# The PSUM ring of the late projections and the odd layer: five banks in five steps

## The chip, the cores and the metric

The kernel runs on one core of a Trainium2 chip. Its time is the device time of one execution in microseconds (us). A core has a matrix engine (TensorE, PE in the profile; PEld is its weight load), a vector engine (VectorE, DVE), a scalar engine (ScalarE, ACT), a general engine (GpSimd, POOL), a queue of DMA issues (SyncE, SP), and DMA engines beside them. Matmuls write their sums to PSUM, eight banks of 512 fp32 columns on 128 partitions; DVE and ACT read the sums from there.

## The reference

One step of a two-layer network on 1024 latent tokens and 256 context tokens of width 1024 (DEPTH = 2). Layer 0 is the even layer (attention), layer 1 the odd one (Fourier mixing); then a final norm.

```python
for l in range(DEPTH):
    hc = modulate(rms_norm(xc, norm_g[l]), shc, scc)      # context
    hl = modulate(rms_norm(xl, norm_g[l]), shl, scl)      # latent
    if l % 2 == 0:   # combined projection; global and windowed attention; SiLU gates; output projection
        yc, ka, va, kb, vb = even_ctx(hc, ...)
        yl = even_lat(hl, ...)
    else:
        yc = odd_mix(hc, odd_w_in[i], odd_w_out[i])
        yl = odd_mix(hl, odd_w_in[i], odd_w_out[i])
    xc = xc + gtc * yc
    xl = xl + gtl[:, None] * yl

def odd_mix(h, w_in, w_out):
    u, gate = jnp.split(h @ w_in, 2, axis=-1)
    return (fourier_mix(u) * jax.nn.silu(gate)) @ w_out   # fourier_mix: Re(FFT2) over positions and 256 channels
```

All values are fp32. The kernel splits each fp32 operand into a high and a low part and makes three matmuls of each product.

## The kernel before

The ten tiles of 128 tokens are projected, normalised and rotated; the queries go through DRAM (`qd`); the attention runs unit by unit (tile, head group, pair of heads), and a filler puts projections and gates between the units. When the last unit is done, `late[0]` becomes true (L1515), and what the filler still holds is run to its end (`fl_.drain()`, L1517).

From there on the sums of every large product come from one function, `next_bank`, which takes the next tag of a ring:

```python
BANKS = {"s": 3, "t": 3, "a": 1, "g": 1}
RING = ("g", "s", "a", "s")
...
    ring = deque(RING)

    def next_bank(name):
        ring.rotate(-1)
        return bank(ring[-1], name)
```

The tag "g" stands for one PSUM bank, "a" for one, "s" for three that are given out as they come free, and "t" for three that serve transposes and small sums and are not in the ring. A tile (one 512-column sum) owns its bank from its first matmul to the last instruction that reads it; the next tile of that tag waits until then.

Walking the program gives 91 calls of `next_bank`, in this order. I number them from 0.

- 0 to 13: `oz`, the output projection of the even layer for the seven rows left at L1515 (6, 3, 7, 1, 5, 8, 9), two halves each (L1304); 24 matmuls a tile, read by DVE at L1308.
- 14 to 37: the gates of the odd layer, L1529 to L1584, four steps `c` of two channel tiles `ct`. For each `ct` a tile `g1E` and a tile `g1O` (L1539, 24 matmuls of 512 columns, read by ACT at L1545 and DVE at L1546, L1547 and L1549); at the end of each `c` two tiles `g1c` (L1559, 24 matmuls of 256 columns, read by ACT at L1562 and DVE at L1564 and L1565). In the last `c` the two small sums `ad12p` (L420) of `r2.finish("g")` (L1580) stand between the last `g1O` (call 35) and the two last `g1c` (calls 36 and 37); they ask for the tag "g" by name, outside the ring (L433).
- 38 to 57: `u`, four passes `n` of five tiles (L1805); 24 matmuls a tile over eight chunks `k` of 128 channels. Chunks 0 to 3 and 4 to 7 use weights that are loaded from `wd` (L1607) and split into a high part (L316, ACT) and a low part (L322, POOL). Read by ACT at L1813 and DVE at L1814.
- 58 to 69: `pcc`, `pc`, `ps`, the position sums of the Fourier mixing (L1828, L1854).
- 70 to 90: `of`, the output projection of the odd layer and the final norm (L1304, L1924).

The order of the instructions on each engine is not the program's. A planner (`schedule_with_timeline_sim=True`, L2053) goes through them with its own estimate of time and puts on an engine the earliest instruction of the program whose inputs and whose bank it thinks ready. The engines then run their queues strictly in that order. So a change of banks can move matmuls, evictions and DMA issues of the stages behind it.

Of the kernel before, what the change touches and what calls it, by code (L numbers as in the profile page):

```python
# [82 lines left out]
E_WL, E_VH, E_KEV, E_QEV = "p", "d", "a", "ad"  # L83
BANKS = {"s": 3, "t": 3, "a": 1, "g": 1}
ALIAS = {}
RING = ("g", "s", "a", "s")


class Buf:
# [57 lines left out]
def hybrid_step(ctx: ExitStack, tc: tile.TileContext, I, O):  # L147
# [37 lines left out]

    ring = deque(RING)

# [1873 lines left out]
```

## Time and profile before

| what | value |
|---|---|
| median of 3 runs | 1179.93 us (1179.76 to 1182.26) |
| profiled execution | 1181.93 us, of which its instructions span 1180.1 us |
| mean granted TensorE clock in the profiled execution | 0.995 |
| busy, of the span | PE 98%, PEld 88%, DVE 70%, ACT 48%, POOL 28% |
| matmuls | 8120 |
| stretch in which the ring is in use | about 764 to 1173 us |

The share of PE is made of matmuls whose ends are modelled, so it tells where PE stood still, not how close it is to its peak. The table of stages in the prediction is read in the same way: what a stage can give is its length less PE's busy time in it. Columns of the stage view: stretch, length, then busy us and number of instructions of PE, PEld, DVE, ACT and POOL, the granted TensorE clock, the share of the DMA engines and GB/s.

### The profile page before, as it was taken

The numbers are of one execution on the slowest core, as the hardware profiler recorded it, in microseconds if no ns is written. First come the engines' busy times: TensorE is split into PE (matmuls) and PEld (weight loads), VectorE is DVE, ScalarE is ACT, GpSimd is POOL, SyncE is SP. The second block draws the span as 40 slices with busy tenths as digits, with TensorE's granted clock in tenths as the row PEclk, the third lists the DMA queues.
The fourth block names the chain that finished last, engine by engine and source line by source line (L and its number), as shares of the span: only waits on it lengthen the run. The fifth ranks groups of instructions, "written<-read, shape, count | busy, mean of one in ns | idle before, by whom it ended". The sixth has DMA issues, their size and how long they took to land.

```text
span 1180.1 us, 22034 instructions
## 1 busy us (share of the span) xinstructions
PE 1151.1 (98%) x8120; PEld 1035.5 (88%) x8120; DVE 829.7 (70%) x1996; ACT 570.2 (48%) x1149; POOL 329.8 (28%) x293
## 2 busy tenths in 40 slices
PE   9998999999999999999999989999999999999997
PEld 8797999999999998899989878887777889998886
DVE  3589787877777776678888877776765962468543
ACT  4343466565656655556666674432363234342211
POOL 2345733512222230010110035365221226200001
PEclk9999999999999999999999999999999999999999
DMA  9977412323532232344352587784214426364321
GB/s 368 371 275 256 129 62 68 97 83 101 151 90 79 77 97 85 94 127 117 78 154 78 158 227 211 232 238 162 90 46 143 151 98 181 100 213 146 125 107 54
DMA packets 112592, 168.80 MB, mean 143 GB/s; under 512 B 25946, under 2 KB 63574, under 8 KB 112484
## 3 DMA queue, kind: packets, MB, share of 16 engines
q1 hardware_dynamic: 109972, 158.74, 42.6%
q0 software_dynamic: 2368, 8.39, 2.4%
q8 instruction: 64, 1.05, 0.4%
q14 instruction: 44, 0.36, 0.1%
q10 hardware_dynamic: 144, 0.26, 0.1%
HBM read 123.19 MB, written 44.16 MB: 142 GB/s over the span
## 4 chain that ended last, share of the span: by engine, by line
PE 70%; DMA 13%; DVE 8%; issue 3%; POOL 2%; ACT 2%; SPq 1%; POOLq 0%; DVEq 0%; ACTq 0%
PE of L296 9%; PE av L1114 9%; PE pt L1108 8%; PE ga L296 8%; PE q L296 8%; PE sL L989 5%; PE u L296 5%; PE g1O L296 3%; PE kv L296 3%; PE sC L989 2%; PE g1E L296 2%; PE oz L296 2%; DMA u<-i_x 2%; DMA wd<-u 2%; PE g1c L296 1%
## 5 line engine op out<-in xcount | busy, mean ns | idle before, releaser
L1111 DVE TENSOR_TENSOR pt<-pt,pt 128x512 fp32r<-128x512 f32 (+1 forms) x264 | 170.9, 658 | 40.5 <-ACT pt L316 39.5
L316 ACT ACTIVATE pt<-pt 128x512 fp32r<-128x512 f32 (+1 forms) x265 | 147.5, 576 | 101.8 <-PE pt L1108 56.2
L1114 PE MATMUL av<-pt,u 128*128 128x256 f32 x1008 | 167.5, 290 | 1.4 <-DVE e L1125 0.8
L1108 PE MATMUL pt<-identr,p 128*128 128x128 f32 x1008 | 157.2, 273 | 1.5 <-ACT p L1030 0.8
L296 PE MATMUL q<-w,u 128*128 128x256 f32 x960 | 145.1, 287 | 0.5 <-ACT e L559 0.5
L1114 PEld LDWEIGHTS av<-pt,u 128*128 128x128 f32 x1008 | 139.1, 190 | 5.0 <-DVE e L1125 1.0
L296 PEld LDWEIGHTS q<-w,u 128*128 128x128 f32 x960 | 127.2, 189 | 5.5 <-ACT e L559 0.7
L1030 ACT ACTIVATE p<-p,nm 128x1280 f32<-128x1280 f32 (+1 forms) x80 | 95.4, 1193 | 68.2 <-DVE p L1023 68.0
L1108 PEld LDWEIGHTS pt<-identr,p 128*128 128x128 f32 x1008 | 119.7, 141 | 8.1 <-ACT p L1030 1.0
L296 PE MATMUL ga<-u,w 128*128 128x512 f32 (+1 forms) x576 | 124.4, 360 | 0.8 <-DVE byp L1085 0.5
L296 PEld LDWEIGHTS ga<-u,w 128*128 128x128 f32 x576 | 93.8, 188 | 15.4 <-ACT pt L316 1.2
L322 POOL TENSOR_TENSOR w<-h,w 128x512 fp32r<-128x512 f32 x38 | 50.0, 1331 | 134.6 <-DVE w L318 106.6
L989 PE MATMUL sL<-u,q 128*128 128x512 f32 x256 | 82.3, 409 | 0.0
L1030 ACT ACTIVATE p<-p,NM 128x640 f32<-128x640 f32 (+2 forms) x80 | 59.2, 740 | 31.5 <-DVE p L1023 31.2
L989 PE MATMUL sC<-u,q 128*128 128x256 f32 x320 | 62.1, 294 | 2.3 <-DMA q<-qd 2.0
L1023 DVE TENSOR_SCALAR_CACHE_REDUCE p<-sL 128x512 f32<-128x512 f32 x64 | 43.8, 685 | 22.3 <-PE sL L989 14.0
L1023 DVE TENSOR_SCALAR_CACHE_REDUCE p<-sL,nm 128x512 f32<-128x512 f32 x64 | 47.7, 745 | 13.9 <-PE sL L989 12.8
L296 PE MATMUL oz<-u,w 128*128 128x512 f32 x192 | 56.4, 399 | 0.4 <-DVE e L1125 0.4
L759 POOL TENSOR_TENSOR h<-h,rope 128x512 f32<-128x512 f32 (+1 forms) x18 | 21.6, 1199 | 121.4 <-ACT h L842 79.2
L989 PEld LDWEIGHTS sC<-u,q 128*128 128x128 f32 x320 | 48.8, 189 | 5.9 <-issue 2.6
L322 POOL TENSOR_TENSOR u<-h,u 128x512 fp32r<-128x512 f32 x16 | 21.0, 1323 | 109.1 <-ACT u L316 81.2
L296 PE MATMUL of<-u,u 128*128 128x512 f32 x150 | 48.2, 393 | 0.0
(735 smaller groups left out, 2590.7 us busy)
## 6 DMA issues: line engine op xcount, KB each, us to landing
q<-qd SPq DMA_DIRECT2D x80, 256.0 KB
h<-i_w_in SPq DMA_DIRECT2D x40, 256.0 KB
h<-i_w_out SPq DMA_DIRECT2D x32, 256.0 KB
p<-i_ada_s SPq DMA_DIRECT2D x11, 512.0 KB
qd<-pt SPq DMA_DIRECT2D x20, 256.0 KB
qd<-q SPq DMA_DIRECT2D x18, 256.0 KB
w<-i_wuT SPq DMA_DIRECT2D x8, 512.0 KB
u<-i_x SPq DMA_DIRECT2D x8, 512.0 KB
```

Of the source, the lines that this page charges most:

```text
L296: last = pe.matmul(out, a, b, start=i == 0, stop=i == n - 1)
L316: return act.activation(out, in_, AF.Copy)
L322: return pick("lo" + lc, lc).tensor_sub(dst_l, src, dst_h)
L759: pick("rope", XE["rope"]).tensor_mul(t1.rearrange("p t h (b c) -> p t (h b) c", b=2), y.rearrange("p t h (b c) -> p t (h b) c", b=2), cb)
L989: pe.matmul(ps, q_at(q, s, hc), keys, start=s == 0, stop=s == 1)
L1023: dve.tensor_scalar(p[i][:, end[i] : end[i] + n], ps, sign, last[i], op0=ALU.mult, op1=ALU.min, accum_out=c)
L1030: act.activation(p[i][:, 0 : end[i]], p[i][:, 0 : end[i]], AF.Exp, bias=last[i], scale=-1.0, accum_out=SU[:, t, hd + i, 0:1],)
L1108: pe.transpose(tp[:, jj * 256 + i * P : jj * 256 + i * P + P], p[i][:, off : off + P], ident)
L1111: dve.tensor_sub(pt[:, 1, 0:n], tp[:, 0:n], pt[:, 0, 0:n])
L1114: pe.matmul(acc, vv, pt[:, s, jj * 256 : jj * 256 + 256], start=c + jj + s == 0, stop=c + jj == nt - 1 and s == 1,)
```

## The change

One constant gets a fifth step:

```diff
-RING = ("g", "s", "a", "s")
+RING = ("g", "s", "a", "s", "s")
```

Before, calls 0, 4, 8, ... take "g", calls 2, 6, 10, ... take "a", and every second call takes one of the three banks of "s". A bank of "g" or "a" comes back after four calls, a bank of "s" after six on average. Now "g" has calls 0, 5, 10, ..., "a" has calls 2, 7, 12, ..., and the other three of each five take "s": every bank comes back after five calls. The number of banks, the sums, the number of instructions and the DMAs stay the same.

## The prediction

> **What bounds the kernel now.** I read the page first, for the share of PE, then the view of stages, for where PE stands still once the ring is in use.
>
> ```profile
> span 1180.1 us, 22034 instructions
> PE 1151.1 (98%) x8120; PEld 1035.5 (88%) x8120; DVE 829.7 (70%) x1996; ACT 570.2 (48%) x1149; POOL 329.8 (28%) x293
> ```
>
> ```profile
> 770.00:850.00 80.00, 79.26 (x371) 64.49 (x370) 57.73 (x76) 22.39 (x44) 41.14 (x23) 1.00 0.52 167
> 850.00:910.00 60.00, 56.92 (x299) 46.06 (x298) 36.47 (x80) 32.81 (x74) 17.45 (x15) 1.00 0.26 88
> 910.00:980.00 70.00, 70.00 (x385) 59.79 (x384) 54.04 (x100) 20.69 (x39) 18.73 (x15) 1.00 0.40 131
> 980.00:990.00 10.00, 8.58 (x70) 8.20 (x69) 2.06 (x6) 3.94 (x9) 6.61 (x9) 1.00 0.73 219
> 990.00:1045.00 55.00, 55.00 (x517) 53.24 (x516) 22.73 (x75) 19.86 (x57) 16.99 (x13) 1.00 0.38 116
> 1045.00:1172.75 127.75, 127.75 (x644) 107.71 (x644) 77.83 (x133) 32.78 (x61) 7.73 (x11) 1.00 0.38 133
> ```
>
> The reader is to see that PE bounds every stage that uses the ring. Length less busy time leaves 0.74 us idle in 770 to 850, 3.08 in 850 to 910, 1.42 in 980 to 990, and nothing elsewhere. The change removes no instruction, so it can give at most these 5.24 us, and only the part of them that is a wait for a bank, or could be filled if another bank were free. The waits of PE after 765 us name them (who waited, for whom, us in all, times, longest):
>
> ```profile
> PE u L296 <- ACT u L316: 1.3, 1, 1.3
> PE g1c L296 <- ACT u L1330: 0.9, 2, 0.5
> PE g1E L296 <- DVE h L1565: 0.9, 1, 0.9
> ```
>
> Only the third is a wait for a bank as such: a `g1E` tile waits for the last reader of a `g1c` tile (L1565). The first is a wait for weights (L316 splits them), and what matters there is whether PE has other work.
>
> **The change part by part.** *The wait at 908 us.* It is call 22 (`g1E3`, tag "a") waiting for call 18 (`g1c0`, "a"). In the new ring call 22 still has "a", but the tile before it there is call 17 (`g1O1`), drained early.
>
> ```profile
> 906.91 0.28 PE L296 MATMUL g1c<-u,u 128*128 128x256 f32 x1
> 908.05 0.93 PE L296 MATMUL g1E<-w,u 128*128 128x512 f32 x3 [0.87 <-DVE h L1565]
> ```
>
> I count nothing for it all the same. When PE stops at 906.91 all five banks are taken: calls 18 and 19 (`g1c`, which wait for the context's transposes) and three finished tiles of the step `c` = 1. Before, these three are calls 20, 21 and 23, and 22 comes last; after, they are 20, 21 and 22, and 23, on an "s" bank, comes last and waits for the same readers. The work of three 24-matmul tiles is the same. What goes is the place of the wait, not its length. Bounds: all of it goes (0.87 less), or nothing; I take nothing, because the five banks are full in both orders.
>
> *The wait at 982 us.* Here PE runs out of ready matmuls before the second half of the first `u` weights is split:
>
> ```profile
> 969.62 1.09 PE L420 MATMUL ad12p<-h,ones 128*2 128x512 f32 x4
> 970.55 0.40 PE L296 MATMUL g1c<-u,u 128*128 128x256 f32 x2
> 973.39 0.28 PE L296 MATMUL u<-w,w 128*128 128x258 f32 x1
> 981.38 0.28 PE L296 MATMUL g1c<-u,u 128*128 128x256 f32 x1
> 982.93 0.63 PE L296 MATMUL u<-u,u 128*128 128x258 f32 x3 [1.27 <-ACT u L316]
> 983.71 0.36 PE L296 MATMUL u<-w,w 128*128 128x258 f32 x1
> ```
>
> The 24 matmuls of a `g1c` tile from 970.55 to 973.39 give 0.118 us a matmul. So PE's work ends at 981.38 + 0.12 = 981.50, and it starts again at 982.93: 1.43 us lost. It then does three matmuls (to 983.39) and waits until 983.71, 0.32 us, for call 40 (`u02`, "g"), whose bank is held by call 36 (`g1c6`, "g") until its reader is through:
>
> ```profile
> 983.28 0.28 DVE L1565 TENSOR_TENSOR h<-g1c,h 128x128 f32<-128x128 f32 x1
> ```
>
> Together 1.75 us. What PE lacked were banks: of the five `u` tiles only calls 38, 39 and 41 had run their first chunks (0 to 3, 12 matmuls, 1.42 us each). Call 40 stood behind `g1c6`, and call 42 ("a") behind call 38 ("a"), which needs the late weights itself. In the new ring call 36 has an "s" bank and call 37 has "a"; call 40 is behind `ad12p` alone, and call 42 behind call 37, the other `g1c` tile. Then the first chunks of calls 40 and 42 are ready too: 24 matmuls, 2.84 us, more than the 1.75 us lost. If the planner puts them ahead, PE has work until 981.50 + 2.84 = 984.34.
>
> *What the new ring adds there.* "g" now also has call 35, `g1O7`, the tile just before `ad12p`, which asks for "g" by name. Before, the tile ahead of `ad12p` on "g" was call 32 (`g1E6`), drained with the first row; now it is `g1O7`, drained with the second:
>
> ```profile
> 958.35 0.41 DVE L1547 TENSOR_TENSOR h<-g1E,h 128x256 f32<-128x256 f32 x1
> 971.09 0.16 DVE L1549 TENSOR_SCALAR h<-g1O 128x1 f32<-128x1 f32 x1
> ```
>
> So `ad12p` cannot start at 969.62 any more, but at 971.25 at the earliest: 1.63 us later. PE fills that time with calls 36 and 37 if they stand ahead in its queue. But others wait for `ad12p`, in this order: the DMA issue of `wd` pieces on SP, the landing, POOL, then SP again with the piece of the late weights, its landing, and the split:
>
> ```profile
> SPq L1607 <- PE ad12p L420: 8.8, 3, 5.5
> ```
>
> ```profile
> 970.74 5.72 SPq L1607 DMA_DIRECT2D h<-wd  x4
> 976.56 0.46 SPq L1555 DMA_DIRECT2D g1d<-u  x1
> 977.11 0.39 SPq L1607 DMA_DIRECT2D w<-wd  x1
> ```
>
> ```profile
> 973.69 0.10 POOL L1609 MEMSET h<- 128x4 f32 x1 [7.69 <-DMA h<-wd]
> 973.80 2.28 POOL L322 TENSOR_TENSOR h<-u,h 128x512 fp32r<-128x512 f32 x1
> 982.95 1.30 POOL L322 TENSOR_TENSOR u<-w,u 128x516 fp32r<-128x516 f32 x1
> ```
>
> ```profile
> 982.24 0.63 ACT L316 ACTIVATE u<-w 128x516 fp32r<-128x516 f32 x1 [4.09 <-DMA w<-wd]
> ```
>
> SP stands for 8.8 us behind `ad12p` between 965 and 975 us; the first of its four `h<-wd` issues at 970.74 starts POOL's memset at 973.69, POOL's 2.28 us finish the operand of the last `ad12p` matmul, and the piece `w<-wd` is issued at 977.11 behind all that. If the whole chain moves by 1.63 us, the high parts come at 982.87 + 1.63 = 984.50 and the low parts at 984.25 + 1.63 = 985.88. PE, with work until 984.34, waits 0.16 us, runs five matmuls of high parts (0.59 us) and waits 0.79 us for the low ones: 0.95 us idle in place of 1.75, a gain of 0.80. If the chain does not move, the gain is 1.75; if it moves and nothing is filled in, PE idles 1.63 us longer. I take the gain of 0.80: the wait for `g1O7` follows from the ring alone, and the rows show SP waiting for `ad12p`. The filling matmuls hide the wait; without them the next thing late is the low part.
>
> *The rest.* `oz` changes banks from call 4 on, but PE is idle 0.74 us in that stage, and its one bank wait there is for the last reader of an attention sum (L1125) on "a", which call 2 has in both rings:
>
> ```profile
> PE oz L296 <- DVE e L1125: 0.4, 1, 0.4
> ```
> The position sums change too: `ps3` (call 69) now comes after `pc1` (call 64) on "s", and `pc3` goes ahead of it. PE has `of` matmuls to run there and stands still nowhere after 990 us, so I count nothing. Bounds for the planner's rearrangements in 770 to 910: all 0.74 + 3.08 us of idle time gone, or, as the nearest row for a loss, one more wait like the 1.63 us one.
>
> The sum is −0.80 us on the profiled execution's 1181.93 us (span 1180.1, so 1.83 us lie around it), that is 1181.1. That execution is 2.00 us above the median of 1179.93; the same 0.80 us off the median gives **1179.1 us**.
>
> **The rivals.**
>
> *Faster.* The chain does not move, because the planner puts `w<-wd` ahead of what waits for `ad12p`, and the order at 908 us loses its wait as well: 1.75 + 0.87 = 2.62 us, 1177.3. For it: both waits are named in the rows. Against it: the full banks at 906.91 and SP's 8.8 us.
>
> *Nothing happens.* PE's queue has the same stalls in other places and the late weights set 982.93 as before: 1179.9. For it: the number of banks is the same, and the largest wait is for weights, not for a bank.
>
> *Slower.* The chain moves by 1.63 us and the planner, which goes by its own estimate, does not put calls 40 and 42 ahead. Then PE idles 1.43 + 1.63 = 3.06 us in one piece. What such a piece does to the clock the trace shows once, earlier:
>
> ```profile
> 749.50:753.08 3.58, 1.57 (x10) 1.20 (x11) 3.57 (x12) 3.32 (x8) 0.45 (x1) 1.00 0.95 286
> 753.08:756.49 3.41, 3.41 (x16) 3.21 (x15) 3.38 (x9) 3.36 (x9) 0.27 (x1) 0.50 0.16 50
> 981.00:984.40 3.40, 1.98 (x15) 1.60 (x14) 0.49 (x2) 2.15 (x5) 3.32 (x5) 1.00 1.07 314
> ```
>
> After a stretch with PE busy 1.57 of 3.58 us the granted clock was 0.50 for 3.41 us; around the present wait, with 1.98 of 3.40, it stayed at 1.00. So somewhere between 1.4 and 2.0 us of idle time in such a stretch the clock halves, and 3.06 us are past that. Half a clock for 3.41 us costs 1.71 us of matmuls: 1.63 + 1.71 = 3.34 us, 1183.3. It decides as soon as less than about 1 us of the 2.84 us of filling work is ahead in the queue.
>
> A page of the Trainium skill ("TensorE: Matmul & The Clock Gate", section "What's actually happening") has a stricter rule: the clock falls to half after at least one idle window of about 3.4 us. By that rule 3.06 us would not halve it, and the slower case would be 1179.93 + 1.63 = 1181.6, within 0.2%. The trace does not agree: at 753 us the clock fell after a stretch in which PE was busy for 1.57 of 3.58 us. So I keep the price with the halved clock.
>
> **How the numbers follow.** Forecast (filled, chain moved) 0.40, nothing 0.12, faster 0.25, slower 0.23. 0.2% is 2.36 us, about what a measurement of this kernel can tell from no change; the forecast and the second rival lie within it, 1177.3 and 1183.3 outside. So faster 0.25, same 0.52, slower 0.23. The likeliest time is 1179.1. The range runs from 1176.6, the faster case with 0.74 us of the idle time of 770 to 850 gone as well, to 1183.4, the slower case; cases of both signs hold much of the chance, and the forecast's own range is 1178.2 (gain 1.75) to 1179.9.
>
> **What would show it.** In the changed trace: `ad12p` at 971.3 or later behind or amid two `g1c` tiles; 60 matmuls of `u` on chunks 0 to 3 (now 36) before the first one that waits for L316; idle time in 980 to 990 under 1 us; a wait of about 0.9 us for L1565 near 907, now ahead of a `g1O` tile. I am wrong if `ad12p` still starts right behind `g1O7`, if `w<-wd` is issued at 977.1 or before, if a stretch at 0.50 clock follows 985 us, or if the stages from 770 to 910 change by over 1 us.

## The result, and the profile after

The changed kernel takes 1191.15 us (median of 5 runs, 1189.5 to 1191.73) against 1181.75 us for the kernel before in the same session (5 runs, 1179.76 to 1186.27): a ratio of 1.0076, with an interval of 1.0054 to 1.0097. It is slower by some 9 us, and above the upper end of the predicted range. The profiled execution took 1191.73 us. Ratios, here and below, leave out two executions of later kernels (1892.57 us of e2 and 1255.45 us of e4), whose mean granted clock was 0.556 and 0.849. The page of the changed kernel begins:

```profile
span 1189.9 us, 22037 instructions
PE 1154.1 (97%) x8120; PEld 1039.0 (87%) x8120; DVE 832.3 (70%) x1996; ACT 570.3 (48%) x1149; POOL 327.9 (28%) x293
```

The work is the same (8120 matmuls), so the 9.8 us of extra span are time in which PE stood still or was clocked down. The view of stages of the changed kernel has the columns used before:

```profile
770.00:850.00 80.00, 75.82 (x349) 61.96 (x348) 61.04 (x76) 21.51 (x40) 41.87 (x24) 0.98 0.53 174
850.00:910.00 60.00, 59.28 (x312) 48.81 (x310) 34.30 (x71) 32.20 (x70) 18.11 (x15) 1.00 0.26 86
910.00:980.00 70.00, 68.52 (x354) 58.08 (x354) 54.56 (x106) 19.80 (x41) 16.14 (x12) 0.98 0.35 117
980.00:990.00 10.00, 10.00 (x78) 9.02 (x76) 3.08 (x7) 4.67 (x10) 4.33 (x6) 1.00 0.81 247
990.00:1045.00 55.00, 50.53 (x469) 48.06 (x469) 20.73 (x67) 18.90 (x53) 19.82 (x21) 1.00 0.37 110
```

Two stages that had no idle time to speak of now have 4.18 us (770 to 850, before 0.74) and 4.47 us (990 to 1045, before 0). The idle time that the change was to remove (980 to 990, before 1.42) is gone, also in the changed kernel's own time, which is 6.22 us behind at that place: PE's first stop after 980 us comes at 1000.67. The waits of PE after 765 us name the new ones (who waited, for whom, us in all, times, longest):

```profile
PE eoE L1341 <- DVE p L1442: 4.1, 1, 4.1
PE u L296 <- ACT u L316: 2.5, 1, 2.5
PE u L296 <- DVE nyr L1816: 1.4, 1, 1.4
...
PE g1O L296 <- DVE h L1565: 0.9, 1, 0.9
PE u L296 <- POOL u L322: 0.6, 1, 0.6
```

For what follows I put the trace's matmuls against the kernel's own list of instructions, which gives each its tile, and cut the time at the same four matmuls in every run: the first of `oz60` (call 0), the last of the `oz` tiles, the last of `g1O7` (call 35), the last of the `u` tiles. Before: 764.25, 850.92, 969.40, 1044.37. After: 765.57, 857.09, 975.62, 1054.15. So the changed kernel is 1.32 us behind when the ring begins, where both kernels still have the same order of instructions on PE; it loses 4.85 us in the `oz` stretch (91.52 for 86.67), 0.05 in the gates (118.53 for 118.48), 3.56 in the `u` stretch (78.53 for 74.97) and nothing behind it. 1.32 + 4.85 + 0.05 + 3.56 = 9.78 us. The gates are equal by luck: the changed kernel has a stretch at half clock there (the 0.98 in its row 910 to 980), which costs 1.7 us, and 0.9 us less of idle time and 0.8 us less of PE's busy time in the rest of that stretch.

**The `oz` loss.** PE's timeline in the kernel before, near 800 us (start, us, then as in the prediction):

```profile
798.01 0.64 PE L1114 MATMUL av<-pt,u 128*128 128x256 f32 x4
798.48 0.62 PE L296 MATMUL oz<-u,w 128*128 128x512 f32 x2
...
803.83 0.40 PE L296 MATMUL oz<-u,u 128*128 128x512 f32 x1
804.06 0.53 PE L1341 MATMUL eoE<-identr,p 128*128 128x128 f32 x3
```

and in the changed kernel:

```profile
799.34 0.63 PE L1114 MATMUL av<-pt,u 128*128 128x256 f32 x4
804.12 0.90 PE L1341 MATMUL eoE<-identr,p 128*128 128x128 f32 x3 [4.15 <-DVE p L1442]
```

Both wait for the same thing, the row `p` that DVE finishes at L1442 at about 804.0 us. Before, the 24 matmuls of `oz50` (call 8, on "g") stood in that time and the wait could not be seen. After, `oz50` is on "s" and starts at 812.28. What the hole did to the clock (the view of stages again, two stretches of the changed kernel):

```profile
799.70:804.10 4.40, 0.27 (x3) 0.06 (x1) 4.40 (x3) 0.65 (x2) 3.28 (x3) 1.00 0.18 63
804.10:807.60 3.50, 3.46 (x9) 2.59 (x10) 3.50 (x5) 1.07 (x1) 0.00 (x0) 0.51 0.32 94
```

After the hole the granted clock is 0.51 for 3.5 us, which costs 3.5 × 0.49 = 1.7 us. With the 3.44 us of added idle time in the stage (4.18 less 0.74) that is 5.1 us, near the 4.85 measured.

**The `u` loss.** PE's timeline of the changed kernel in the second pass (`u10` to `u14`):

```profile
999.28 1.38 PE L296 MATMUL u<-u,w 128*128 128x258 f32 x10
1002.04 1.87 PE L296 MATMUL u<-u,w 128*128 128x258 f32 x12 [1.38 <-DVE nyr L1816]
1006.38 0.74 PE L296 MATMUL u<-u,u 128*128 128x258 f32 x4 [2.47 <-ACT u L316]
1007.74 1.46 PE L296 MATMUL u<-u,u 128*128 128x258 f32 x10 [0.63 <-POOL u L322]
```

First a tile waits for a bank (L1816 is the last reader of a `u0` tile), then PE waits for the second half of this pass's weights. SP issues these late; its queue in the kernel before and in the changed one (start, length of the issue, waits for buffers included):

```profile
990.00 0.33 SPq L1170 DMA_DIRECT2D h<-i_w_out  x1
991.55 0.37 SPq L1607 DMA_DIRECT2D pt<-wd  x1
```

```profile
996.52 4.83 SPq L1170 DMA_DIRECT2D h<-i_w_out  x3
1001.44 0.39 SPq L1607 DMA_DIRECT2D pt<-wd  x1
```

Measured from the last matmul of `g1O7`, `pt<-wd` is issued after 22.2 us before and after 25.8 us now, behind three loads of `w_out1`, of which one stood there before. So there are two suspects in this stage: banks, since all five `u0` tiles are now open together, and the order on SP.

### The profile page after: what moved, and what is told of

It is laid out like the page before. It is cut to its first block, busy times and chain, and to the rows that moved or that the text cites. A ratio compares the mean times of both kernels' runs of the same rounds, so it can differ in the third digit from the quotient of the medians.

```text
span 1189.9 us, 22037 instructions
## 1 busy us (share of the span) xinstructions
PE 1154.1 (97%) x8120; PEld 1039.0 (87%) x8120; DVE 832.3 (70%) x1996; ACT 570.3 (48%) x1149; POOL 327.9 (28%) x293
## 4 chain that ended last, share of the span: by engine, by line
PE 79%; DMA 9%; DVE 5%; ACT 2%; issue 2%; POOL 2%; SPq 1%; POOLq 0%; DVEq 0%; ACTq 0%
PE of L296 9%; PE av L1114 9%; PE ga L296 8%; PE pt L1108 8%; PE q L296 8%; PE oz L296 6%; PE sL L989 5%; PE g1E L296 4%; PE g1O L296 4%; PE u L296 3%; PE sC L989 3%; PE kv L296 3%; PE g1c L296 2%; DMA u<-i_x 2%; PE sB L1061 1%
## 5 line engine op out<-in xcount | busy, mean ns | idle before, releaser
L316 ACT ACTIVATE pt<-pt 128x512 fp32r<-128x512 f32 (+1 forms) x265 | 147.3, 575 | 101.2 <-PE pt L1108 55.5
L322 POOL TENSOR_TENSOR w<-h,w 128x512 fp32r<-128x512 f32 x38 | 49.9, 1330 | 134.7 <-DVE w L318 106.4
L322 POOL TENSOR_TENSOR u<-h,u 128x512 fp32r<-128x512 f32 x16 | 22.8, 1430 | 112.2 <-ACT u L316 107.3
```

The costliest lines, as they stand in the source:

```text
L316: return act.activation(out, in_, AF.Copy)
L322: return pick("lo" + lc, lc).tensor_sub(dst_l, src, dst_h)
```

## The experiments

Each kernel below takes the tags of the 91 calls from a list; `old[n]` is `("g", "s", "a", "s")[n % 4]` and `new[n]` is `("g", "s", "a", "s", "s")[n % 5]`. Their line numbers differ by one to three from those above, so L315 and L316, or L1815, L1816 and L1819, are the same line. Every ratio is to the kernel before, run on the same chip in the same session; it is not the quotient of the two medians, and for e2 (1.0052 by the medians) and e5 (1.0029) the two differ by over a thousandth. The execution that is profiled is one of 5 to 12, and they scatter by several us ahead of the ring already (`oz60` starts between 756.3 and 765.6 us in the profiles), so the stretches tell more of what a change did than the time of that one execution. Some stretches hold time at half clock; the last column has what it cost them.

| run | median us (before) | ratio, interval | `oz` stretch | gates | `u` stretch | half clock in it |
|---|---|---|---|---|---|---|
| before | | | 86.67 | 118.48 | 74.97 | none |
| after | 1191.15 (1181.75) | 1.0076, 1.0054 to 1.0097 | 91.52 | 118.53 | 78.53 | `oz` 1.7, gates 1.7 |
| e1 | 1181.51 (1178.30) | 1.0028, 1.0014 to 1.0041 | 86.09 | 120.19 | 80.36 | gates 1.7, `u` 1.7 |
| e2 | 1184.45 (1178.30) | 1.0038, 1.0016 to 1.0059 | 87.55 | 116.81 | 77.44 | `u` 1.7 |
| e3 | 1183.20 (1178.30) | 1.0039, 1.0018 to 1.0059 | 86.80 | 116.96 | 80.52 | `u` 3.4 |
| e4 | 1185.10 (1178.30) | 1.0048, 1.0027 to 1.0070 | 93.66 | 116.82 | 74.76 | `oz` 3.4 |
| e5 | 1183.15 (1179.76) | 1.0042, 1.0027 to 1.0057 | 85.41 | 118.20 | 76.84 | none |
| e6 | 1178.25 (1179.76) | 0.9993, 0.9974 to 1.0013 | 85.41 | 118.15 | 73.69 | none |
| e7 | 1183.84 (1179.76) | 1.0031, 1.0012 to 1.0049 | 86.79 | 118.41 | 77.90 | `u` 1.7 |
| e8 | 1179.94 (1179.76) | 1.0002, 0.9989 to 1.0016 | 86.08 | 118.63 | 76.69 | `u` 1.7 |
| e9 | 1175.25 (1177.30) | 0.9982, 0.9961 to 1.0003 | 85.90 | 118.60 | 73.14 | none |
| e10 | 1176.88 (1177.30) | 0.9987, 0.9965 to 1.0008 | 86.96 | 118.55 | 73.77 | gates 1.7 |
| e11 | 1177.78 (1177.97) | 1.0004, 0.9984 to 1.0025 | 85.86 | 119.39 | 73.37 | none |

### Two losses or one: e1 and e2

```diff
-RING = ("g", "s", "a", "s")
+RING = [old[n] if n < 14 else new[n] for n in range(91)]   # e1
+RING = [new[n] if n < 14 else old[n] for n in range(91)]   # e2
```

> Calls 0 to 13 (the `oz` tiles) take their banks from the old ring, calls 14 to 90 from the new one. Theory (two separate losses: `oz50` held behind `oz10`, and the `u1` pass): the idle 4.4 us and the half clock near 800 to 808 us are gone, the stage from 990 us stays as in the changed kernel (about 50.5 us of PE work up to 1045 us, waits for L316 and L1816 there), and the time is 3 to 4.5 us over the kernel before. Rival (the whole loss is made in the `oz` stage and the later one follows from it): the time is within 1 us of the kernel before. Rival (all of it comes from call 14 on): the full 9 us over the kernel before.

> Calls 0 to 13 take their banks from the new ring, calls 14 to 90 from the old one (whose next step after call 13 is the same as in the kernel before). Theory (two separate losses): the tile `oz50` comes behind `oz10`, PE stands idle some 4.3 us near 800 us with a half clock behind it, the stage from 990 us is as in the kernel before, and the time is 4 to 6 us over the kernel before. Rival (all from call 14 on): within 1 us of the kernel before.

Measured by the ratios, e1 is 3.3 us over the kernel before (0.0028 × 1178.30) and e2 4.5 us. Together that is 7.8 us, within the interval of the whole change (1.0054 to 1.0097, 6.4 to 11.5 us). In e1 the `oz` stretch is that of the kernel before and the waits of the second `u` pass are all there; in e2 the second pass has no wait. So there are two losses, and neither follows from the other.

The profiled execution of e2 shows a hole of only 1.31 us, with no half clock behind it, and it is one of its quickest (1177.91 us). The reason is in the operand that PE waits for. DVE, and POOL beside it, in the changed kernel:

```profile
798.69 3.40 DVE L1427 SCALAR_TENSOR_TENSOR p<-w,r11y,p 128x1024 f32<-128x1024 f32 x1
802.01 2.05 DVE L1442 TENSOR_TENSOR p<-w,pt 128x1024 f32<-128x1024 f32 x1
```

```profile
798.57 2.44 POOL L1284 TENSOR_TENSOR u<-u,u 128x1024 f32<-128x1024 f32 x1 [2.85 <-DMA u<-gd]
```

and in the profiled execution of e2:

```profile
791.78 1.28 DVE L1426 SCALAR_TENSOR_TENSOR p<-w,r11y,p 128x1024 f32<-128x1024 f32 x1
792.98 1.22 DVE L1441 TENSOR_TENSOR p<-w,pt 128x1024 f32<-128x1024 f32 x1
```

```profile
792.01 4.42 POOL L1283 TENSOR_TENSOR u<-u,u 128x1024 f32<-128x1024 f32 x1 [3.20 <-DMA u<-gd]
```

The same two DVE instructions take 3.40 + 2.05 or 1.28 + 1.22 us: 2.95 us decided by whether POOL's instruction starts 0.12 us ahead of DVE's or 0.23 us behind it, in which case POOL's is the long one. Without cover, this race is paid by PE.

### Why `oz50` came late: e3 and e4

My theory was that the tiles of one tag get their banks in the order of the calls, also when a bank of that tag is free. In the changed kernel `oz50` (call 8) follows `oz10` (call 6) on "s". The high and the low part of `oz50`'s row are ready by 795.72 (POOL, L318) and 796.98 (DVE, L322), those of `oz10`'s row only by 802.98 and 809.00. The first matmul of `oz10` is at 811.81 and that of `oz50` at 812.28, though the banks that the two took had been free since 783.5 and 788.6. In the kernel before, `oz10` was on "a" and `oz50` on "g", behind nothing.

```diff
+RING = [new[n] for n in range(91)]                 # e3
+RING[5], RING[8] = RING[8], RING[5]
+RING = [old[n] for n in range(91)]; RING[6] = "g"  # e4
```

> The new ring in all calls, but calls 5 and 8 have changed places: `oz71` is on one of the three `s` banks and `oz50` on `g`, as `oz50` is in the kernel before. Theory (a tile is not placed before the tile of the same tag that was asked for earlier, even when banks are free, so `oz50` is held behind `oz10`): `oz50` runs near 798 to 804 us again, the idle 4.4 us there and the half clock behind it are gone, the `u1` loss stays: 3 to 4.5 us over the kernel before, some 5 us less than the changed kernel. Rival (the `oz` stage loses by the banks' distance in general, not by `oz50` on `s`): the idle time stays within 1 us of 4.4 us, and the time is that of the changed kernel, 8 to 10 us over the kernel before.

> The old ring with one call changed: call 6 (`oz10`) takes `g` in place of `a`, so `oz10` and `oz50` (call 8) follow each other on `g`. Theory (order of asking within a tag): `oz50` cannot run before `oz10` has been placed and evicted, PE stands idle over 4 us near 800 us with a half clock behind it, and the time is 4 to 8 us over the kernel before. Rival (the loss needs the new ring's distances, or the number of free banks): within 1 us of the kernel before.

PE's timeline in e3 (the first fence) and in e4 (the second):

```profile
790.67 0.64 PE L1114 MATMUL av<-pt,u 128*128 128x256 f32 x4
791.15 0.62 PE L296 MATMUL oz<-u,w 128*128 128x512 f32 x2
...
796.73 0.49 PE L1341 MATMUL eoE<-identr,p 128*128 128x128 f32 x3
```

```profile
795.15 0.63 PE L1114 MATMUL av<-pt,u 128*128 128x256 f32 x4
801.50 0.90 PE L1341 MATMUL eoE<-identr,p 128*128 128x128 f32 x3 [5.72 <-DVE p L1442]
```

With the whole new ring and one pair exchanged, the tile is back in the hole. With the whole old ring and one tag changed the hole is there, larger than in the changed kernel: in e4 the bank of "g" was free from 790.03 on, and `oz50` was put on it at 823.53, after `oz10` had come and gone. The times are about as expected: 4.6 and 5.7 us over the kernel before by the ratios, where 3 to 4.5 and 4 to 8 were expected. e3 keeps the `u` loss and has a stop of 1.2 us of its own at 822 us, and its interval still overlaps that of the changed kernel, so what the exchange gives back is shown by the timeline and not by the time. In all 13 traces, the tiles of calls 0 to 57 that are on the ring start in the order of the calls within each tag, without an exception. So "given out as they come free", as the section on the kernel before has it for "s", holds only in this order: a tag is a queue, with its banks as servers, and whoever is not ready holds up those behind.

### The `u` pass: e5 to e8

e5, e6 and e8 start from e1 (old up to call 13, new from 14), e7 from the kernel before.

```diff
-            r2.finish("g")
+            r2.finish("t")                          # e5, e7
+RING[42], RING[43] = RING[43], RING[42]             # e6
...
-                sp.dma_start(raw.a, src[k * P : (k + 1) * P, sl])
+                ld = sp.dma_start(raw.a, src[k * P : (k + 1) * P, sl])   # e8
+                for first in lows.get("wd", []):
+                    queue_behind(ld, first)
...
+            if (c, hf) == (0, 1):                   # e8, in u_gap: ld is the load from wd
+                lows.setdefault("wd", []).append(ld)
```

> Calls 0 to 13 old, 14 to 90 new, and the two `ad12p` sums take their bank from `t` in place of `g`, so that they no longer stand behind `g1O7`'s or in front of `u02`'s use of that bank. Against the run with calls 14 to 90 new, whose PE stood idle 1.51, 2.79 and 0.78 us in the `u1` pass (waits for L1815, L315 and L321 there). Theory (the `u1` loss is for want of banks and for the second weight pieces coming late, whatever `ad12p` does): idle time of at least 2.5 us stays in the `u1` pass; the time is 0 to 3 us over the kernel before. Rival (the late `ad12p` and the chain of SP and GpSimd behind it delay the weights, and so make the loss): the idle time there falls under 1 us and the time is 1 to 3 us below the kernel before.

> Calls 0 to 13 old, 14 to 90 new, but calls 42 and 43 have changed places: `u04` is on one of the `s` banks and has to wait for `u00`'s, `u10` is on `a`, which is free early. Only four `u0` tiles can be open at once, and `u04`'s 24 matmuls stand whole behind the others, as in the kernel before. Theory (the fifth open tile is what costs: its work is used up as cover early, and `u10` to `u14` find no bank): of the 5.1 us of idle time in the `u1` pass at least 3.5 go, and the time is 2 us below to 0.5 us over the kernel before. Rival (the loss is only for the weight pieces `pt`, `q`, `w` from `wd` that are issued late): the wait for L316 of 2.6 us or more stays, and the time is 2 to 4 us over the kernel before.

> The old ring in all calls; only the two `ad12p` sums take their bank from `t`. It is the ring-free way to the gain that the change was to have at 981 to 984 us (1.43 and 0.32 us of idle time in the kernel before). Theory (`ad12p` between the last gate tiles on `g` keeps `g1c6` and `u02` back, and the rest of the stage stays as it is): the idle time at 981 to 984 us falls under 0.5 us, no new wait in the `u1` pass, 1 to 2 us below the kernel before. Rival (what is gained there is lost at the next wait for weights from `wd`): within 0.7 us of the kernel before.

> Calls 0 to 13 old, 14 to 90 new, and on SP's queue the loads of `w_out1` stand behind the four loads from `wd` of `u_load(1)`; the order on the other engines is unchanged. The load `pt<-wd` comes some 4.9 us earlier than in the run with calls 14 to 90 new (3 loads of `w_out1` held SP from 984.25 to 989.08 us there). Theory (late second pieces are half the loss, the banks the other half): the wait for L315 of 2.79 us and the one for L321 of 0.78 go, the one for L1815 of 1.5 us stays or moves: 0 us within 1.5 of the kernel before. Rival (the banks alone): the idle time only moves to other waits, and the time stays 2.5 to 4 us over the kernel before.

e6 removes the whole `u` loss. Its stage from 980 us:

```profile
980.00:1045.00 65.00, 65.00 (x597) 62.75 (x596) 27.34 (x90) 24.67 (x68) 18.74 (x20) 1.00 0.44 137
```

One exchanged pair, which keeps `u04` from holding the fifth bank, takes the `u` stretch from 80.36 us in e1, 1.7 of them half clock, to 73.69. `u04` then runs its 24 matmuls whole behind the four others, from 985.07 us on, and PE has them while the next weights come. But with the banks the planner's order on SP has changed as well; in e6 `pt<-wd` goes ahead of the loads of `w_out1`:

```profile
984.75 0.36 SPq L1607 DMA_DIRECT2D pt<-wd  x1
...
988.52 5.41 SPq L1170 DMA_DIRECT2D h<-i_w_out  x3
```

That is 20.3 us after the last matmul of `g1O7`, where e1 has 26.0. So e6 changes both suspects, and cannot tell what the fifth open tile costs by itself.

e8 leaves the banks as they are and changes only the order of SP's queue, and `pt<-wd` goes ahead of the loads of `w_out1` here too; PE, ACT, DVE and POOL keep the order of e1:

```profile
987.87 0.36 SPq L1608 DMA_DIRECT2D pt<-wd  x1
...
990.53 7.89 SPq L1169 DMA_DIRECT2D h<-i_w_out  x5
```

The waits for the weights (2.6 and 0.6 us in e1) are gone, the waits for a bank stay (for L1816, 1.6 us in all, with half a clock behind them), and the time is that of the kernel before; the `u` stretch, 76.69 us, is still 1.72 us over it, about what the half clock costs. So the late pieces are the larger part of the loss, 3.2 us of waits in e1, and that is shown. That the five open tiles, which use up the cover early, are needed for these waits too is likely and not shown: no run has four open tiles and pieces as late as those of e1. The smaller part, the waits for a bank, stands in e8 with the pieces early.

e5 has the theory's idle time in the `u` pass (a wait of 2.5 us for L315, one of 0.5), so the late `ad12p` is not the cause of the wait for weights; the wait of 1.4 us for a bank that e1 has is not there. Its time, 5.0 us over the kernel before by the ratio and 3.4 by the medians, is above what either theory gave, and more than its `u` stretch of 76.84 us (1.87 over) accounts for; that rest is not explained.

e7 is a miss of both theories, 3.7 us over the kernel before: the wait at 981 us does go, to 0.3 us, but a larger one comes after it.

```profile
PE u L295 <- DVE nyr L1815: 2.4, 1, 2.4
```

```profile
990.65 1.17 DVE L317 CAST h<-h 128x512 fp32r<-128x512 f32 x1 [9.45 <-DMA h<-i_ctab]
991.74 0.28 DVE L1813 TENSOR_TENSOR u<-u,u 128x128 fp32r<-128x128 f32 x1
```

`u04` needs "a" from `u00`, whose last matmul is at 987.66. But on DVE the planner has put the split of a table (L317) ahead of `u00`'s eviction, and that split stands for its DMA until 990.65.

### The mended ring, and the new ring in its useful part: e9 and e10

```diff
+RING = [new[n] if 14 <= n < 38 else old[n] for n in range(91)]   # e9
+RING = [new[n] for n in range(91)]                               # e10
+RING[5], RING[8] = RING[8], RING[5]
+RING[42], RING[43] = RING[43], RING[42]
```

> Only the gate tiles (calls 14 to 37) take their banks from the new ring; the `oz` tiles before them and everything from `u00` on take them as in the kernel before. Theory (the new ring pays between `g1O7` and `u0`, where it lifts `g1c6` and `u02` off the bank of `ad12p`, and costs only in the `oz` tiles and where `u04` opens early): no idle time of over 0.5 us from 970 to 1010 us, the time from the last matmul of `g1O7` to the last one of the `u` tiles is 73.3 to 73.8 us, where the kernel before has 74.97 and the run with calls 42 and 43 changed has 73.69, and the time is 0.5 to 2 us below the kernel before. Rival (the banks of `u0` and `u1` under the new ring are needed for that gain too): the wait for L316 near 982 us is back with 1 us or more, and the time is within 0.5 us of the kernel before.

> The new ring in all calls with two pairs exchanged, 5 with 8 and 42 with 43, so that `oz50` does not follow `oz10` on `s` and `u04` does not hold a fifth bank. Theory (those two places are the whole loss of the changed kernel): 1 us below to 1 us over the kernel before; the idle 4.4 us near 800 us and the 5 us in the `u1` pass are both gone, and the stretch from the last matmul of `g1O7` to the last one of the `u` tiles is 73.3 to 74.0 us. Rival (the new ring costs in other places as well): 3 us or more over the kernel before.

With two pairs exchanged the whole new ring is at 0.9987: the 9 us are gone with two places. The new ring does cost a little in a third one: the stop at 822 us that e3 has is there, with 1.3 us. With the new ring only for the gates, the `u` stretch is 73.14 us, 1.83 less than before, with no idle time in it:

```profile
980.00:1045.00 65.00, 65.00 (x601) 63.23 (x600) 29.70 (x90) 24.56 (x68) 18.86 (x21) 1.00 0.45 139
```

Its time is 2.1 us below the kernel before, but the interval (0.9961 to 1.0003) reaches past 1; that it is faster is likely and not shown. By the intervals it does beat the changed kernel (1.0054 at the least), as e6, e8, e10 and e11 do.

### The wait at 908 us: e11

e9, with the two tiles that hold banks while they wait for the context moved off the ring:

```diff
-                ps = next_bank(f"g1c{ct}")[:, 0:256]
+                ps = next_bank(f"g1c{ct}") if ct > 1 else (ring.popleft(), t_bank(f"g1c{ct}"))[1]
+                ps = ps[:, 0:256]
```

> As the run with only the gate tiles on the new ring, and `g1c0` and `g1c1` take their banks from `t`, so that five banks stay for the gate tiles while those two wait for the context's transposes. Theory (the wait for L1565 near 902 to 908 us is there because two of the five ring banks are held by `g1c0` and `g1c1`, as the prediction argued; it goes when they hold none, and PE then also has work while ACT's L1330 splits the context): the idle time in that place, 1.0 us for L1565 and up to 1.9 us for L1330 and L1548 in the run before this one, falls under 0.8 us together, the stretch from the last matmul of the `oz` tiles to the last one of `g1O7` is 116.3 to 117.5 us in place of 118.5, and the time is 2 to 4.5 us below the kernel before. Rival (what is waited for is the context's rows, whatever the banks are): the stretch stays within 0.5 us of 118.5 us, and the time is that of the run before this one, 1 to 2.5 us below the kernel before.

A miss of both: the wait for L1565 goes, but two others come, and the gates take 119.39 us in place of 118.60.

```profile
PE g1E L295 <- DVE h L1548: 1.6, 1, 1.6
PE g1E L295 <- ACT w L1524: 1.4, 1, 1.4
```

The second stands at 907 us, the first at 940. Freeing two banks here, at the price of two of the three banks of `t`, only moved the stop to other tiles.

## Why the prediction was wrong, by its own steps

**The wait at 908 us, counted at nothing: right, for the place and the length of the wait.** It is there with the same 0.9 us, ahead of a `g1O` tile as said. That the gates also take the same time in both kernels (118.48 and 118.53 us) is luck, since the second has the half clock in it. The reason given, five full banks, is half of it: e11 freed two of them, and this wait went, but two others came and nothing was won.

**The wait at 982 us, counted at a gain of 0.80 us: right in kind, too small.** All of the 1.75 us went; e9's `u` stretch is 1.83 us shorter. (The size of that wait is itself not firm: with the same tags from call 14 on, PE waits there for 1.3 us in the kernel before, 2.3 in e2 and 0.7 in e4.) The term that was mis-sized is the chain of SP, POOL and DMA behind `ad12p`, which was to move by 1.63 us. `ad12p` did move, by more than that, to a place amid the last `g1c` tile:

```profile
979.87 1.09 PE L420 MATMUL ad12p<-h,ones 128*2 128x512 f32 x4
```

But the late weights stand behind less of it:

```profile
981.00 0.37 SPq L1607 DMA_DIRECT2D h<-wd  x1
981.42 0.50 SPq L1607 DMA_DIRECT2D w<-wd  x1
```

The first load still waits for `ad12p`: it comes 0.04 us after the end of the four matmuls (980.96), and by the kernel's list of instructions it is these that it waits for. But it is the only load between them and `w<-wd`; before there were four, with POOL's work among them, and three of the four wait for the second `ad12p` sum. So the first `w<-wd` is issued 5.80 us after the last matmul of `g1O7` (975.62), where it was 7.71 us (977.11 less 969.40): 1.91 us earlier in place of 1.63 later. The planner took the other order, which the prediction had as its bound of 1.75. (Set back by the 6.22 us that the changed kernel is behind, the issue stands at 975.20; "at 977.1 or before" was one of its signs of being wrong.) Ahead of the late weights PE ran 48 matmuls of the first chunks, where 36 stood before and 60 were forecast. The halved clock of the slower rival did not come here.

**"`oz` changes banks from call 4 on, but PE is idle 0.74 us in that stage", and so counted at nothing: this step failed, for 4.85 us in the profile and 4.5 by e2's ratio.** The prediction's own sign for it, that the stages from 770 to 910 change by over 1 us, did come. The step looked at the waits that the stage had, and asked which of them the new ring would change. It did not ask what hid the waits that could not be seen. PE ran `oz50` for 5.6 us (798.48 to 804.06) just when DVE had row `p` to finish; it could do so because "g" had no unready tile in front of it. The list of the calls and their tags, with the rows in the order 6, 3, 7, 1, 5, 8, 9, shows it without a run of the new kernel: row 1 comes before row 5 in the calls and after it on PE, and in the new ring both ask for "s".

**"PE has `of` matmuls to run there and stands still nowhere after 990 us, so I count nothing": this step failed too, for 3.3 us net (e1).** It weighed the position sums and passed over the second `u` pass. Of the 24 filling matmuls that were counted as a gain at 982 us, 12 were taken out of `u04`, which before ran whole from 991.86 to 994.73 as cover for the next weights, and `u04` held the fifth bank meanwhile. Both follow from the prediction's own sentence that calls 40 and 42 run ahead; it was not carried on to the next wait. The late issue of `pt<-wd`, without which e8 has no wait for weights, does not follow from it: that is the planner's new order on SP, which the prediction followed only to the issue at 977.11.

**The bounds.** That "it can give at most these 5.24 us" was sound; for the loss the nearest row was "one more wait like the 1.63 us one", and that is where the range became too narrow. The idle time of a stage bounds what can be won there, not what can be lost. What was lost here were waits that had been covered (4.15 us, behind the 5.6 us of `oz50`), waits that the planner's new order brought, and half a clock behind some of them, 1.7 us each time.

## What to carry to other kernels

Before banks or buffers are dealt out anew, write down for each tag the order in which its tiles are asked for and the order in which they become ready: where a late one stands before an early one on the same tag, the early one is lost as cover, however many banks are free. Work that fills one hole is taken from the next one, so follow a tile that is pulled ahead to the place where it used to run. And a stage that has no idle time can still lose: cost it by the waits that its full engine hides, and add a half clock that may follow.

## What the runs showed of the hardware

**Where a hole falls decides on the clock, and not its length alone.** In each of the 13 traces, every stretch at half clock begins at a point of one grid with a step of 3.41 us, and all but the last, which runs to the end of the trace, are one or two steps long. Where the grid lies differs from execution to execution. The wait for the late weights is 2.5 us in the changed kernel and 2.6 in e1. In the changed kernel two steps of the grid share it, and the clock stays:

```profile
1002.09:1005.51 3.42, 1.82 (x12) 1.50 (x12) 0.36 (x3) 0.45 (x2) 0.00 (x0) 1.00 0.92 261
1005.51:1008.92 3.41, 1.91 (x13) 1.71 (x14) 0.65 (x3) 3.05 (x7) 2.52 (x3) 1.00 0.20 54
```

In e1 the larger part of it and the next wait fall into one step, and the step behind has half a clock:

```profile
992.71:996.12 3.41, 1.25 (x8) 1.04 (x9) 0.29 (x1) 2.56 (x7) 1.85 (x2) 1.00 0.34 94
996.12:999.53 3.41, 3.41 (x18) 3.41 (x18) 0.36 (x2) 0.49 (x1) 3.41 (x4) 0.50 0.36 99
```

In e8 two waits of 0.2 and 1.4 us in one step were enough:

```profile
990.22:993.64 3.42, 1.82 (x14) 1.46 (x13) 2.73 (x9) 0.84 (x5) 1.35 (x1) 1.00 0.98 300
993.64:997.05 3.41, 3.41 (x18) 3.41 (x18) 0.93 (x5) 2.99 (x8) 2.76 (x3) 0.50 0.29 94
```

Of the steps from 764 to 1150 us in these traces that began at full clock, each of the six with PE busy for at most 1.65 us was followed by half a clock, as were four of the eight with 1.73 to 1.93 us and none with more: 1.4 to 1.8 us of idle time in a step decide it here. So the prediction's threshold, "somewhere between 1.4 and 2.0 us of idle time in such a stretch", is near the truth for a step of the grid, and does not hold for a stretch laid anywhere. (It says that the trace of the kernel before shows a halved stretch once ahead of this; there is a second one, from 39.69 to 43.11 us.) The Trainium skill ("TensorE: Matmul & The Clock Gate", section "What's actually happening") has the clock judged by a free-running window of about 3.4 us, so that the same hole can fall within one window or across two; these rows agree with that. The rule of the same section that one whole idle window is needed does not agree with e1, where PE was busy for 1.25 us of the window ahead of the half clock, or with e8, where it was busy for 1.82.

**DVE and POOL shut each other out for whole instructions.** L1427 takes 1.28 us when it starts 0.23 us before POOL's L1284 (in e2) and 3.40 when POOL's has started 0.12 us before it (in the changed kernel); POOL's takes 2.44 us or, when it is the later one, 4.42, with this DVE instruction and the next inside its time. The Trainium skill ("SBUF — State Buffer", section "Who interferes with whom") says that a DVE instruction with two SBUF inputs contends with a GpSimd instruction that reads SBUF, and that the order of issue decides who blocks; these four durations agree. That some of the scatter of this kernel from run to run comes from such races is likely; no run here shows it.
